# Feed-forward output of layer 0: where the seventh product's weights are added up, and where two bank copies and a table load stand

## The chip, the cores and the metric

The kernel runs on one core of one Trainium2 chip. The metric is the time of one execution on the device in microseconds; before the change the median of three runs is 1351.96 us (1351.9 to 1352.2). The profile is of one further execution, which took 1352.66 us; from its first to its last instruction (its span) it took 1350.7 us. Where a text says TensorE, VectorE, ScalarE, GpSimd and SyncE, the profile says PE (PEld for its weight loads), DVE, ACT, POOL and SP; a q behind the name is the engine's own instruction queue, which also issues transfers.

## The reference, cut to what matters

The program is a trunk of two layers for 256 latent tokens and 256 context tokens of width 1024. Each layer has a token mixer (an mLSTM in layer 0, latent attention in layer 1) and a gated feed-forward part; both are followed by a layer norm of the residual. The change is in the output product of the feed-forward part of layer 0 and at the norm behind it:

```python
def _conv_ffn(h, w_in, conv_w, conv_b, w_out):
    gate, up = jnp.split(h @ w_in, 2, axis=-1)
    return (jax.nn.silu(_dwconv(gate, conv_w, conv_b)) * up) @ w_out
...
f = _conv_ffn(_modulate(x, ml[3], ml[4]), ...)
x = _layer_norm(ALPHA * x + ml[5] * f, ln_g[i, 1], ln_b[i, 1])
```

w_out has 2816 rows and 1024 columns. The same is done for the context tokens, xc. All values are float32.

## The kernel before, in words

**Products in three passes.** A float32 operand is split into a high half, which ScalarE makes by a cast to fp32r, and a low half, which VectorE makes by subtracting the high half from the source. A product of two such operands is three matmuls: high by high, high by low, low by high (mm3, L420 to L427). In prod (L1655) the activations are the first operand, so the second matmul of each three (L426) is the first that needs the weights' low half.

**The weight stream.** Weights come in tiles of 128 rows by 1024 columns (512 KB). Class Stream goes through one fixed list of them (order, made by _plan). _load (L294) takes a raw buffer from a ring and issues the load on SyncE's queue; _split (L320) has ScalarE cast the tile into the high half (L342) and, through low (L362), VectorE subtract for the low half (L364), after which the raw buffer is given back and the next load is issued. use (L371) hands a tile to the products and first splits tiles ahead, as long as fewer than three (NB) of the w buffers are in use: the cast of a tile so waits until the tile three places ahead of it has been used up. From the first y tile on the ring has eleven raw buffers, from y22 on seven. SyncE works its queue in order; a load that waits for its buffer holds up all loads behind it.

**Seven products instead of eight.** The output product of layer 0 (w_fout0, L1629) is computed in blocks of 2 by 2: two blocks of weight rows in each pair, two halves of columns, two groups of 256 tokens, with seven block products and sums of operands on both sides. For each of six groups of rows (the last of half size, 512 columns) there are tiles yt2, y11, yt3, yt1, then in three more passes y21, y22 and yt4. The weights' sums are formed on the chip by _sum (L310): of the loaded tiles for yt3, yt1 and y11 VectorE makes T2 and the others in place (L316, L317, L318). T2 takes a raw buffer but no load. yt4 needs T4, the sum of T2 and B21 (the block that y21 also uses; ws holds it under yt4's number). So T2 is spilled: _split stores it into a tile of memory, t2d, by a transfer on ScalarE's queue (L344). When yt4's turn comes, _load reads t2d back on SyncE's queue (L302) and then adds B21 onto it by an accumulating transfer from GpSimd's queue (L303). The value projection of the mLSTM (w_v, tiles v...) does the same and keeps doing it.

**The activation side.** act_sums (L1607) is called for each of the eleven pairs of feed-forward rows, j = 0 to 10, while the input product (ffn_in, L1558) is still running. It forms sums, splits some of them, and stores the parts that are wanted later in a memory tile fd by two transfers on GpSimd's queue (L1618, L1624). In w_fout0 the step operand (L1638) brings them back: loads of 128 KB on ScalarE's queue (L1644, tile zr), and two steps later a cast on ScalarE (L1650) and a subtraction on VectorE (L1651, tile fz).

**The banks.** Four pairs of PSUM banks hold the running products: p6 (yt2), p1 (y11), p7 (yt3), p5 (yt1). When p1's six tiles are through, ScalarE copies its two banks into u1 (L1698); VectorE then adds p6 (L1705), adds the result to p7 (L1708) and so on (sums, L1703). p1 then takes y21, p5 takes y22, p7 takes yt4, each on top of what it holds. add (L1718) multiplies a finished bank by the gate, adds the residual z and takes statistics for the norm. z and the gate are loaded on GpSimd's queue (L1692, L1686). The norm of the context rows (z_norm, L1773) follows in the course of yt4: a square root on ScalarE (L1780), scaling on both engines (L1784, L1786), transposes on TensorE (L1271), then scale and shift and the split into hc (L1277, L1278, L1284, L1285), on which the first product of layer 1 (dkv, L1808) waits.

**What sets the order.** A planner takes the instructions as traced and gives each engine a fixed order: of the instructions that are ready by its own clock, the one traced first. Three helpers bind it. keep_in_program_order puts an instruction behind the last one traced so far on its engine. behind (L429) puts one behind named instructions of the same engine, in order only, without a wait for their end. st.behind lists instructions that the next splits must stand behind. Each transfer takes one of eight counters for those issued on SyncE's and ScalarE's queues, or one of eight for those on GpSimd's; an issue waits until the counter's last transfer has landed.

Of the kernel before, what the change touches and what calls it, by code (L numbers as in the profile page):

```python
# [10 lines left out]
AF = mybir.ActivationFunctionType  # L11
ALU = mybir.AluOpType
# [244 lines left out]
class Stream:  # L257
# [36 lines left out]
    def _load(self):  # L294
        k, j = self.k, self.nl
        key = self.order[j][0]
        n, cols = self.ids[key]
        j0, ring = self.ring(j)
        tag, bufs = ring[(j - j0) % len(ring)]
        t = k.pool.tile([128, CW], F32, tag=tag, name="raw", bufs=bufs)  # L300
        if key[0] in ("vt4", "yt4"):
            k.nc.sync.dma_start(t[:, :cols], k.t2d[key[0][0], key[1], key[2]][:, :cols])  # L302
            k.nc.gpsimd.dma_start(t[:, :cols], self.ws[n, :, :cols], accum_op=ALU.add)  # L303
        elif key[0] not in ("vt2", "yt2"):
            k.nc.sync.dma_start(t[:, :cols], self.ws[n, :, :cols])
        self.raw[j] = t
        self.tags[j] = tag
        self.nl += 1
# [11 lines left out]
    def _split(self):  # L320
        k, j = self.k, self.ns
        key, wide = self.order[j]
        cols = self.ids[key][1]
        while self.nl <= j:
            self._load()
        self.nsum = max(self.nsum, j)
        while self.nsum < min(j + SUMS, self.n):
            while self.nl <= self.nsum:
                self._load()
            self._sum(self.nsum)  # L330
            self.nsum += 1
        raw = self.raw[j]
        if wide:
            h, l = self.unit(), None
            if self.later is None:
                l = self.unit()
        else:
            w = k.pool.tile([128, 2, CW], F32R, tag="w", name="w", bufs=NB)
            h, l = w[:, 0], w[:, 1]
            self.live.append(j)  # L340
        src = raw[:, :cols]
        k.behind(k.nc.scalar.copy(h[:, :cols], src), self.behind)  # L342
        if key[0] in ("vt2", "yt2"):
            k.nc.scalar.dma_start(k.t2d[key[0][0], key[1], key[2]][:, :cols], src)  # L344
        self.hl[j] = [h, l]
        self.ns += 1
        if l is None:
            self.later.append((j, src, self.hl[j]))
        elif key[0] == "dkv" and key[2]:
            self.kept_low.append((j, src, h, l))  # L350
        else:
            self.low(j, src, h, l)
        while self._room():
            self._load()
# [39 lines left out]
class K:  # L394
# [1212 lines left out]
    def act_sums(self, j, x1, x2):  # L1607


        nc = self.nc  # L1610
        a, b = slice(0, 256), slice(256, 512)
        if j == 0:
            self.fa, self.fd = {}, []
        d = self.dr.tile([128, 768], F32, name="fd")
        t = self.s2("fs")
        nc.vector.tensor_sub(t[:, a], x1[:, b], x2[:, b])
        nc.vector.tensor_sub(t[:, b], t[:, a], x1[:, a])
        nc.gpsimd.dma_start(d[:, 0:512], x2)  # L1618
        nc.vector.tensor_sub(x1[:, b], x1[:, a], x1[:, b])
        u, v = self.u("fa"), self.u("fs")  # L1620
        self.split(u[:, 0], u[:, 1], x1)
        self.split(v[:, 0], v[:, 1], t)
        nc.vector.tensor_add(x1[:, a], x2[:, a], t[:, b])
        nc.gpsimd.dma_start(d[:, 512:768], x1[:, a])  # L1624
        self.fa["1", j], self.fa["S3", j] = u[:, :, a], u[:, :, b]
        self.fa["S1", j], self.fa["S2", j] = v[:, :, a], v[:, :, b]
        self.fd.append(d)

    def w_fout0(self, x1d, mid):  # L1629


        nc, st, A = self.nc, self.st, self.fa
        pin = self.tc.keep_in_program_order
        parts = [("2", i) for i in range(6)] + [("S4", i) for i in range(6)] + [("3", i) for i in range(6)]
        off = {"2": 0, "3": 256, "S4": 512}
        got = []

        def operand():  # L1638
            if parts:
                x, i = parts.pop(0)  # L1640
                r = self.s2("zr")
                js = [j for j in (2 * i, 2 * i + 1) if j < 11]
                for h, j in enumerate(js):
                    pin(nc.scalar.dma_start(r[:, h * 256:(h + 1) * 256], self.fd[j][:, off[x]:off[x] + 256]))  # L1644
                got.append((x, js, r))
            if len(got) > 2 or not parts and got:
                x, js, r = got.pop(0)
                n = 256 * len(js)
                u = self.u("fz")
                pin(nc.scalar.copy(u[:, 0, :n], r[:, :n]))  # L1650
                nc.vector.tensor_sub(u[:, 1, :n], r[:, :n], u[:, 0, :n])  # L1651
                for h, j in enumerate(js):
                    A[x, j] = u[:, :, h * 256:(h + 1) * 256]

        def prod(ps, x, w, i, bs=(0, 1), on=False):  # L1655
            for h in range(2 if i < 5 else 1):
                j = 2 * i + h
                a = A[x, j]
                for b in bs:
                    ts = slice(b * 128, (b + 1) * 128)  # L1660
                    cs = slice(h * 512, (h + 1) * 512)
                    self.mm3(ps[b], (a[:, 0, ts], a[:, 1, ts]), (w[0][:, cs], w[1][:, cs]), j == 0 and not on, j == 10, on)

        def pair():
            return [self.ps("y") for _ in range(2)]

        lo, hi = slice(0, 512), slice(512, 1024)
        p6, p1, p7, p5 = [pair() for _ in range(4)]
        n = 0
        u2 = []  # L1670
        for i in range(6):
            for name, ps, x in (("yt2", p6, "S2"), ("y11", p1, "1"), ("yt3", p7, "S3"), ("yt1", p5, "S1")):
                w = st.use((name, 0, i))
                prod(ps, x, w, i)
                for f in ("S2", "1", "S3", "S1"):
                    if f == x:
                        for j in (2 * i, 2 * i + 1):
                            A.pop((f, j), None)
                self.tick(1)
                if n >= 8:  # L1680
                    operand()
                if n == 14:
                    gate = []
                    for g in (1, 0):
                        t = self.uf("gate")
                        nc.gpsimd.dma_start(t, self.gd[0, 5][g:g + 1, :].to_broadcast([128, 1024]))  # L1686
                        gate.append(t)
                if n >= 16 and n % 2 == 0:
                    if n == 16:
                        z = []  # L1690
                    t = self.uf("z")
                    nc.gpsimd.dma_start(t, x1d[len(z)])  # L1692
                    z.append(t)
                n += 1
                if (name, i) == ("y11", 5):
                    for b in range(2):
                        u = self.s2("u1")
                        pin(nc.scalar.copy(u, p1[b]))  # L1698
                        u2.append(u)
        stats = [self.tiny(12, "st").rearrange("p (a b) -> p a b", b=6) for _ in range(4)]  # L1700
        vv = []

# [15 lines left out]
        def add(g, c, ps, bs=(0, 1)):  # L1718

            for b in bs:  # L1720
                t = self.s2("zp")
                zz = z[2 * g + b][:, c]
                nc.vector.tensor_tensor(t, ps[b], gate[g][:, c], op=ALU.mult)
                nc.vector.scalar_tensor_tensor(zz, zz, ALPHA, t, op0=ALU.mult, op1=ALU.add)
                nc.vector.bn_stats(stats[2 * g + b][:, c.start // 512], zz)
# [7 lines left out]
        for i in range(6):  # L1733
            w = st.use(("y21", 0, i))
            prod(p1, "2", w, i, on=True)
            self.tick(1)
            operand()
# [3 lines left out]
        for i in range(6):  # L1741
            w = st.use(("y22", 0, i))
            prod(p5, "S4", w, i, on=True)
            self.tick(1)
            operand()
        self.drain()
        add(0, hi, p5)
        self.bg = [mid(0, z[0:2], stats[0:2])]
# [514 lines left out]
```

## Time and profile before

| | us |
|---|---|
| median of three runs | 1351.96 |
| the profiled execution | 1352.66 |
| its span | 1350.7 |
| TensorE busy (matmuls) | 1338.8 |
| VectorE busy | 1058.7 |
| ScalarE busy | 711.3 |
| GpSimd busy | 124.7 |

In the profile a line of a group or of the timeline names the source line, the engine, the operation and what it writes and reads (out<-in), with sizes as partitions by elements. Timeline rows begin with the start and the duration in us, and end in brackets with the engine's idle time before the row and what ended it. Rows of waits give who waited for whom: us in total, times, longest. Rows of windows give a stretch, its length, and for each engine the busy time with the number of instructions in brackets, in the order PE, PEld, DVE, ACT, POOL; then the granted TensorE clock, the mean busy share of the sixteen DMA engines, and GB/s. Rows of the chain of waits give start, duration and what the end waited for. Rows of DMA issues give the number of transfers, the size of each, and the median time from issue to landing.

The input product of layer 0's feed-forward part runs up to 922 us, the products of w_fout0 from there to about 1038, interleaved at their end with the first products of layer 1.

### The profile page before, as it was taken

The page shows a single profiled execution, that of the slowest core. Times are in us where ns is not written, and L with a number is a line of the kernel's source. Part 1 is how long each engine was busy: PE and PEld are TensorE (multiplying, and loading weights), DVE is VectorE, ACT ScalarE, POOL GpSimd, SP SyncE. Part 2 cuts the span into 40 slices and gives each one's busy share as a digit, 9 for nine tenths or more (in the row PEclk, how much of TensorE's full clock was granted, in tenths as well). Part 3 has the DMA queues.
Part 4 walks back from the last instruction along what each step waited for, and adds up shares of the span by engine and source line. Part 5 has one row for each costly group of instructions (what it writes and reads, how often), then busy time and mean ns, then how long its engine had stood idle before and what let it go on. Part 6 is the DMA issues. An engine that isn't in the chain of part 4 may idle for free.

```text
span 1350.7 us, 18775 instructions
## 1 busy us (share of the span) xinstructions
PE 1338.8 (99%) x6662; PEld 1120.2 (83%) x6662; DVE 1058.7 (78%) x1748; ACT 711.3 (53%) x1251; POOL 124.7 (9%) x218
## 2 busy tenths in 40 slices
PE   9999999999999999999999999999999999999997
PEld 6777888888888888888898888888878998988886
DVE  4798656677688697897979878767899788898873
ACT  4765544445734545464643433334557767676660
POOL 0222000011101011030002000000001002000100
PEclk9999999999999999999999999999999999999999
DMA  9888848789676374785627876645987437366750
GB/s 362 323 278 283 281 162 257 229 280 311 217 251 195 95 248 137 239 300 198 232 84 245 296 244 229 221 142 206 310 255 243 157 102 211 134 210 190 257 193 32
DMA packets 92637, 298.26 MB, mean 221 GB/s; under 512 B 12120, under 2 KB 16472, under 8 KB 92544
## 3 DMA queue, kind: packets, MB, share of 16 engines
q1 hardware_dynamic: 62992, 218.65, 48.5%
q0 software_dynamic: 17888, 58.09, 13.8%
q10 hardware_dynamic: 11664, 20.32, 4.2%
q8 instruction: 52, 0.85, 0.3%
q14 instruction: 41, 0.34, 0.1%
HBM read 263.56 MB, written 33.46 MB: 220 GB/s over the span
## 4 chain that ended last, share of the span: by engine, by line
PE 93%; DMA 3%; DVE 1%; ACT 1%; issue 1%; ACTq 0%; DVEq 0%; POOL 0%; POOLq 0%; SPq 0%
PE fin L1472 8%; PE tok L423 6%; PE fin L423 6%; PE fin L426 6%; PE fin L427 6%; PE tok L426 6%; PE tok L427 6%; PE y L426 5%; PE y L427 5%; PE y L423 5%; PE qk L423 4%; PE qk L427 4%; PE qk L426 4%; PE up L709 2%; DMA raw<-in_ws 2%; PE up L423 1%
## 5 line engine op out<-in xcount | busy, mean ns | idle before, releaser
L342 ACT CAST w<-raw 128x1024 fp32r<-128x1024 f32 (+2 forms) x286 | 296.2, 1037 | 289.7 <-PE fin L427 78.9
L364 DVE TENSOR_TENSOR w<-raw,w 128x1024 fp32r<-128x1024 f32 (+2 forms) x286 | 343.2, 1203 | 133.4 <-ACT w L342 127.8
L537 DVE SCALAR_TENSOR_TENSOR junk<-ar,bc 128x1024 f32<-128x1024 f32 x128 | 155.9, 1218 | 5.0 <-ACT bc L579 3.0
L426 PE MATMUL fin<-h,w 128*128 128x512 f32 (+1 forms) x376 | 141.2, 376 | 0.0
L427 PE MATMUL fin<-h,w 128*128 128x512 f32 (+1 forms) x376 | 140.9, 375 | 0.0
L423 PE MATMUL fin<-h,w 128*128 128x512 f32 (+1 forms) x376 | 140.8, 376 | 0.1
L1472 PE MATMUL fin<-h,w 128*128 128x512 f32 (+1 forms) x636 | 111.1, 337 | 0.0
L1472 PEld LDWEIGHTS fin<-h,w 128*128 128x128 f32 x636 | 97.6, 190 | 13.2
L423 PE MATMUL qk<-xc,w 128*128 128x512 f32 x256 | 100.6, 393 | 0.0
L427 PE MATMUL qk<-xc,w 128*128 128x512 f32 x256 | 99.9, 390 | 0.0
L426 PE MATMUL qk<-xc,w 128*128 128x512 f32 x256 | 99.8, 390 | 0.0
L426 PEld LDWEIGHTS fin<-h,w 128*128 128x128 f32 x376 | 70.8, 188 | 13.1 <-DVE h L1304 0.2
L427 PEld LDWEIGHTS fin<-h,w 128*128 128x128 f32 x376 | 70.8, 188 | 12.8
L423 PEld LDWEIGHTS fin<-h,w 128*128 128x128 f32 x376 | 70.5, 188 | 13.0 <-ACT h L1303 0.3
L427 PEld LDWEIGHTS qk<-xc,w 128*128 128x128 f32 x256 | 48.1, 188 | 9.9
L426 PEld LDWEIGHTS qk<-xc,w 128*128 128x128 f32 x256 | 48.1, 188 | 9.7
L423 PEld LDWEIGHTS qk<-xc,w 128*128 128x128 f32 x256 | 48.1, 188 | 9.7
L423 PE MATMUL tok<-w,hT 128*128 128x512 f32 x128 | 49.9, 390 | 0.0
L426 PE MATMUL tok<-w,hT 128*128 128x512 f32 x128 | 49.8, 389 | 0.0
L427 PE MATMUL tok<-w,hT 128*128 128x512 f32 x128 | 49.8, 389 | 0.0
L726 ACT ACTIVATE fg<-fg 128x512 f32<-128x512 f32 (+1 forms) x44 | 23.1, 525 | 45.5 <-DVE fg L724 39.4
L364 DVE TENSOR_TENSOR wu<-raw,wu 128x1024 fp32r<-128x1024 f32 (+1 forms) x37 | 43.7, 1201 | 3.6 <-ACT wu L342 3.2
(481 smaller groups left out, 3109.2 us busy)
## 6 DMA issues: line engine op xcount, KB each, us to landing
raw<-in_ws SPq DMA_DIRECT2D x282, 512.0 KB, 4.4
ar<-in_adaT SPq DMA_DIRECT2D x80, 512.0 KB, 4.7
adaw<-in_ada SPq DMA_DIRECT2D x16, 512.0 KB, 8.0
t2d<-raw ACTq DMA_DIRECT2D x13, 512.0 KB, 6.0
raw<-t2d SPq DMA_DIRECT2D x13, 512.0 KB, 6.4
raw<-in_ws POOLq DMA_DIRECT2D x13, 512.0 KB, 8.3
zr<-fd ACTq DMA_DIRECT2D x33, 128.0 KB, 4.4
xmd<-xr POOLq DMA_DIRECT2D x16, 256.0 KB, 4.9
```

Of the source, the lines that this page charges most:

```text
L342: k.behind(k.nc.scalar.copy(h[:, :cols], src), self.behind)
L364: i = self.k.nc.vector.tensor_sub(l[:, :n], src, h[:, :n])
L423: q = mm(out, w[0], x[0], start=start, stop=False, skip_group_check=on)
L426: mm(out, w[0], x[1], start=False, stop=False, skip_group_check=on)
L427: mm(out, w[1], x[0], start=False, stop=stop, skip_group_check=on)
L537: nc.vector.scalar_tensor_tensor(o, w, 1.0, self.bc[j], op0=ALU.mult, op1=ALU.mult, accum_out=col[:, k, j:j + 1])
L709: nc.tensor.matmul(ps[m], wk[i][:, c], hT[k][:, j], start=made[m] == 0, stop=made[m] == 23)
L726: nc.scalar.activation(tmp[:, :n], tmp[:, :n], AF.Silu)
L1472: self.nc.tensor.matmul(ps[:, 0:256] if x else ps, w[x][:, k * 128:(k + 1) * 128], h[:, 0:256] if x else h, start=i == 0 and not k0, stop= ...
```

## The change

In _load a yt4 tile is read by one plain load of its t2d tile. In _split the spill of a yt2 tile becomes an accumulating transfer from GpSimd's queue onto t2d. So that there is something to add to, act_sums copies B21, memory to memory, from ws to t2d on GpSimd's queue, in its calls j = 5 to 10 (for yt4's tiles 0 to 5), each pinned behind what GpSimd's queue has so far. The v tiles keep the old way.

The two copies of p1's banks are traced after st.use of tile yt3 5, whose splits hold the cast of y21's tile 0, and no longer ahead of it. And a square root of a constant into an unused tile is put on ScalarE behind the last cast of operand; the table for square roots is loaded with it.

```diff
         t = k.pool.tile([128, CW], F32, tag=tag, name="raw", bufs=bufs)
-        if key[0] in ("vt4", "yt4"):
+        if key[0] == "yt4":
+            k.nc.sync.dma_start(t[:, :cols], k.t2d["y", key[1], key[2]][:, :cols])
+        elif key[0] == "vt4":
             k.nc.sync.dma_start(t[:, :cols], k.t2d[key[0][0], key[1], key[2]][:, :cols])
             k.nc.gpsimd.dma_start(t[:, :cols], self.ws[n, :, :cols], accum_op=ALU.add)
...
         k.behind(k.nc.scalar.copy(h[:, :cols], src), self.behind)
-        if key[0] in ("vt2", "yt2"):
+        if key[0] == "yt2":
+            k.nc.gpsimd.dma_start(k.t2d["y", key[1], key[2]][:, :cols], src, accum_op=ALU.add)
+        elif key[0] == "vt2":
             k.nc.scalar.dma_start(k.t2d[key[0][0], key[1], key[2]][:, :cols], src)
...
         nc.gpsimd.dma_start(d[:, 512:768], x1[:, a])
+        if j > 4:
+            n, cols = self.st.ids["yt4", 0, j - 5]
+            self.tc.keep_in_program_order(
+                nc.gpsimd.dma_start(self.t2d["y", 0, j - 5][:, :cols], self.st.ws[n, :, :cols]))
...
-        got = []
+        got, cut = [], []
...
                 u = self.u("fz")
-                pin(nc.scalar.copy(u[:, 0, :n], r[:, :n]))
+                cut[:] = [nc.scalar.copy(u[:, 0, :n], r[:, :n])]
+                pin(cut[0])
...
                 w = st.use((name, 0, i))
+                if (name, i) == ("yt3", 5):
+                    for b in range(2):
+                        u = self.s2("u1")
+                        pin(nc.scalar.copy(u, p1[b]))
+                        u2.append(u)
                 prod(ps, x, w, i)
...
                 n += 1
-                if (name, i) == ("y11", 5):
-                    for b in range(2):
-                        u = self.s2("u1")
-                        pin(nc.scalar.copy(u, p1[b]))
-                        u2.append(u)
...
             operand()
+        self.behind(nc.scalar.activation(self.tiny(1, "pre"), self.keps, AF.Sqrt), cut)
         self.drain()
         add(0, hi, p5)
```

## The prediction, made before the result was known

> **What bounds the kernel now.** I read the page's busy shares first, then TensorE's own waits, then windows around them, and last the rows of each engine there.
>
> ```profile
> span 1350.7 us, 18775 instructions
> PE 1338.8 (99%) x6662; PEld 1120.2 (83%) x6662; DVE 1058.7 (78%) x1748; ACT 711.3 (53%) x1251; POOL 124.7 (9%) x218
> PE idle L646 <- DVE adav L490: 1.5, 1, 1.5
> PE y L426 <- DVE w L364: 1.0, 1, 1.0
> PE dkv L423 <- ACT hc L1284: 0.8, 1, 0.8
> 940.00:980.00 40.00, 40.00 (x178) 33.14 (x177) 32.70 (x37) 20.81 (x28) 1.62 (x3) 1.00 0.88 305
> 980.00:985.00 5.00, 3.99 (x18) 2.98 (x17) 5.00 (x9) 4.83 (x8) 0.00 (x0) 1.00 0.98 334
> 985.00:1020.00 35.00, 35.00 (x156) 28.93 (x155) 31.48 (x43) 17.37 (x22) 3.89 (x5) 1.00 0.86 249
> 1023.00:1025.00 2.00, 1.20 (x10) 0.96 (x9) 0.93 (x3) 1.97 (x5) 0.00 (x0) 1.00 1.00 244
> 1340.00:1350.70 10.70, 2.75 (x23) 2.54 (x22) 6.75 (x15) 0.44 (x2) 2.85 (x2) 0.83 0.26 98
> ```
>
> TensorE is busy 1338.8 of 1350.7 us. Of the 11.9 us left, 8.0 lie in the tail after 1340 and most of the rest at the start. The change works between about 820 and 1030, where only two waits of TensorE exist: **1.01 us** at 983 (5.00 less 3.99), for the low half of a weight tile, and **0.80 us** at 1024 (2.00 less 1.20), for a high half of the context activations. A change that adds no matmul and removes none can gain these 1.81 us at most, 0.13% of the time. What a measurement of this kernel can tell from no change is about 0.2%, 2.7 us. So a gain that counts isn't there to be had; the open questions are how much of 1.81 comes, and whether something new is late. The profiled execution took 1352.66 us for a span of 1350.7, 0.70 over the median of 1351.96; I take differences from its rows and put them on the median.
>
> **The first wait: the bank copies.** ScalarE and VectorE around it, then TensorE:
>
> ```profile
> 980.07 0.58 ACT L1698 COPY u<-y 128x512 f32<-128x512 f32 x1
> 980.54 0.58 ACT L1698 COPY u<-y 128x512 f32<-128x512 f32 x1
> 981.02 1.06 ACT L342 CAST w<-raw 128x1024 fp32r<-128x1024 f32 x1
> 982.49 1.05 ACT L342 CAST w<-raw 128x1024 fp32r<-128x1024 f32 x1
> 980.91 1.28 DVE L1705 TENSOR_TENSOR u<-y,u 128x512 f32<-128x512 f32 x2
> 982.11 0.69 DVE L1708 TENSOR_TENSOR y<-y,u 128x512 f32<-128x512 f32 x1
> 982.71 1.22 DVE L364 TENSOR_TENSOR w<-raw,w 128x1024 fp32r<-128x1024 f32 x1
> 983.84 0.68 DVE L1651 TENSOR_TENSOR fz<-zr,fz 128x512 fp32r<-128x512 f32 x1
> 983.98 0.50 PE L426 MATMUL y<-w,fz 128*128 128x512 f32 x1 [1.01 <-DVE w L364]
> ```
>
> The cast at 981.02 is y21's tile 0; two copies of p1 stand ahead of it. Moved ahead of them it starts at 980.07 and ends at 981.13, and its subtraction (1.22) can end at 982.35, before TensorE asks for it at 982.97 (983.98 less 1.01). The copies then end at about 982.1, where the cast's end was, so the next cast stays at 982.49. But VectorE has no idle time here (5.00 of 5.00), and the same work must still be done before tile 1's subtraction: L1705 twice, two L1708, one L1651. In the present order that next subtraction comes last and ends at 986.3 (983.84 and two pieces of 0.6 and 1.22 behind it). TensorE asks for it one tile after 982.97 or a little sooner: twelve matmuls at 40.00 us by 178, so 2.7, at about 985.3 to 985.7. So the wait can come back one tile later, up to 1.0 us, if the planner leaves that subtraction last; each 0.6 us piece that falls behind it takes 0.6 off. Bounds of the gain: 0 and 1.01. I take half, **-0.5**, since the subtraction is traced ahead of those pieces but its cast ends only at 983.54.
>
> **The second wait: table, and the two-step loads of T4.** The chain of waits, ScalarE, GpSimd and the page's DMA list:
>
> ```profile
> 1006.02 10.29 DMA raw<-in_ws
> 1016.41 1.95 ACT L342 CAST w<-raw 128x1024 fp32r<-128x1024 f32 x2 [2.24 <-DMA raw<-in_ws]
> 1018.38 1.28 ACT L1780 ACT_TABLE_LOAD   x1
> 1024.02 0.71 ACT L1284 CAST hc<-zm 128x256 fp32r<-128x256 f32 x2
> t2d<-raw ACTq DMA_DIRECT2D x13, 512.0 KB, 6.0
> raw<-t2d SPq DMA_DIRECT2D x13, 512.0 KB, 6.4
> raw<-in_ws POOLq DMA_DIRECT2D x13, 512.0 KB, 8.3
> 1006.02 0.87 POOL L303 DMA_DIRECT2D raw<-in_ws  x1 [0.41 <-DVE w L364]
> 1019.62 2.01 POOL L303 DMA_DIRECT2D raw<-in_ws  x2 [0.39 <-issue]
> ```
>
> A T4 tile now needs a load of T2 (6.4) and, behind it, an accumulating load of B21 (8.3); the third lands at 1016.3 and holds ScalarE's cast for 2.24. Then a table load of 1.28 us stands ahead of the square root, and everything up to the cast of hc at 1024.02 follows in line. After: six accumulating loads leave, and one load of 6.4 us from SP's same six places brings T4 ten microseconds sooner; the cast is then limited by its weight buffer, from about 1013. The table load, with a dummy square root of 0.3, moves behind the last L1650 cast, into the stretch where ScalarE idles (17.37 busy of 35.00 between 985 and 1020). If that cover were gone it would cost 1.6 us of ScalarE there, inside the lead of a cast worked out below. So hc comes at least 1.28 earlier by the table alone, more than the 0.80 that TensorE waits; next late would be TensorE's own transposes, which is no wait. Bounds 0 (if the cast or dkv's casts take the freed place) and 0.80; I take **-0.8**, since two independent removals each exceed it or come near it.
>
> [...]
>
> **The spill: ScalarE's store becomes GpSimd's accumulation.** Rows:
>
> ```profile
> SPq L305 <- DMA t2d<-raw: 34.1, 5, 9.2
> ACT fz L1650 <- DMA raw<-in_ws: 3.5, 2, 2.5
> 961.89 6.15 DMA t2d<-raw
> 968.10 4.40 DMA raw<-in_ws
> 972.52 0.33 ACTq L1644
> 978.89 11.20 SPq L305 DMA_DIRECT2D raw<-in_ws  x6
> 994.74 1.05 ACT L342 CAST w<-raw 128x1024 fp32r<-128x1024 f32 x1 [1.31 <-PE y L427]
> ```
>
> Removed: six issues of 0.33 on ScalarE's queue. Added: six of about 0.87 on GpSimd. No row shows an accumulation into memory; the nearest, into the chip, takes 8.3 against the store's 6.0. I bound it by 6.0 and by 10.3, the slowest row above, and take 8.3, so +2.3 each. Behind it waits SP, in order, since the raw buffer comes free only then: 34.1 us in five waits now, some 46 then. Behind SP's waiting load stand the other loads. They have room: the load issued at 978.89 is y22's first, its cast is at 994.74, and its landing takes about 5, leaving ten. The weak place is the other one: at 972.52 an issue of zr on ScalarE's queue waited until a load of SP had landed that itself had waited for the spill, and the L1650 cast behind it lost 2.5 us. What is +2.3 for the spill can so be +2.3 for ScalarE. Its lead: with three weight buffers a cast starts two tiles (5.4 us) before use and needs 1.06 and 1.22 with the subtraction, which leaves 3; in the last row of half tiles the same gives 1.4; I take 2. Against that, six 6 us transfers leave the queues that zr shares. I count 0 and keep 0 to +2.3 per spill for the rivals. DMA share in that stretch is 0.88 already, so the added traffic pushes it towards 1.
>
> [...]
>
> **The copies of B21.** Six issues on GpSimd, each behind the second store of its L1607 call:
>
> ```profile
> 793.22 0.54 POOL L1618 DMA_DIRECT2D fd<-fg  x1 [16.27 <-DVE fg L1594]
> 929.84 0.54 POOL L1624 DMA_DIRECT2D fd<-fg  x1 [5.54 <-DVE fg L1623]
> 944.96 0.54 POOL L1692 DMA_DIRECT2D z<-x1d  x1 [10.04 <-PE y L427]
> 700.00:900.00 200.00, 200.00 (x884) 165.61 (x883) 162.11 (x257) 77.38 (x133) 15.13 (x28) 1.00 0.71 232
> 973.34 0.33 ACTq L344 DMA_DIRECT2D t2d<-raw  x1
> ```
>
> GpSimd idles 16 us between calls and DMA has 0.29 free. Memory to memory isn't shown; between the 6.4 of a plain load and 10.3 it lands long before its spill: the last is issued after 929.84 for a spill at 973.34. Queued behind the last copy are the gate and z loads, which are used only after the y21 loop, near 998. Cost 0. The spills now stand in the same queue as the z loads, which wait for buffers, 10.04 us in the row above; a spill behind such a load would be late by as much, and SP with it. The planner takes the one that is ready first, so I count 0 for it, and put it with the slower rival.
>
> **Sum.** -0.5 - 0.8 = -1.3: 1351.96 - 1.3 = **1350.7 us** (on the profiled execution, 1351.4).
>
> **Rivals.**
> 1. *VectorE takes the first gain back and more*, or zr lands up to 1 us later: first wait 1 to 2 us, second gone. 1351.96 + 0 to 1.0 - 0.8 = 1351.2 to 1352.2. For it: VectorE 5.00 of 5.00. Against: zr loses the stores ahead of it.
> 2. *Slower: the accumulating spill holds ScalarE.* The last three spills each delay, through SP's load, a zr issue by 2.3 to 4.3 us; once the lead of 2 is gone TensorE pays: 3 x 2.3 - 2 = 4.9, less 0.8 = +4.1, 1356.1; at 4.3 each 10.9 - 0.8, 1362. It decides from a spill landing of 8 us or more if the same zr follows. For it: the rows at 961.89 to 972.52, and DMA at 0.88. Against: the planner spreads loads and zr anew, and between spills ScalarE idles half the time.
> 3. *It doesn't do what it says*: a copy, cast or table load is placed so that both waits stay, 1352.0.
> 4. *More than the waits comes*: nothing in the rows gives over 1.8; some reordering near 1130 or in the tail would have to, 1349.
>
> **Chances.** Forecast (1350.0 to 1351.2) 0.50; rival 1 0.20; rival 2 0.20; rival 3 0.08; more than 2.7 us faster 0.02. Faster by over 0.2% 0.02, within 0.78, slower 0.20. The range runs from all of 1.81 gained less the 0.2 by which single runs differ, 1349.9, up into the lower part of rival 2, where only some of the spills get through, 1355.0; what it leaves out is the rest of rival 2 and rival 4.
>
> **What would show it.** Right: no wait for L1284 near 1023, ACT_TABLE_LOAD before 1000, T4's casts waiting for TensorE instead of DMA, the first wait under 0.6 or moved one tile on. Wrong: TensorE waiting for L364 or L1651 between 945 and 985, ScalarE's waits for raw<-in_ws above 3.5, SP's waits for the spill far above 46, landings of the spill above 10.

## The result, and the profile after

| | before | after |
|---|---|---|
| median, us | 1352.08 (6 runs, 1351.9 to 1353.17) | 1359.84 (6 runs, 1358.97 to 1360.81) |
| the profiled execution, us | 1352.66 | 1358.97 |
| its span, us | 1350.7 | 1356.6 |

The changed kernel is slower: ratio **1.0053**, 95% interval 1.0042 to 1.0063, or 7.8 us between the medians. The prediction was 1350.7 us.

Windows of the changed kernel, with the same columns and mostly the same bounds as those shown of before:

```profile
940.00:980.00 40.00, 38.98 (x173) 31.97 (x171) 29.84 (x33) 18.05 (x23) 5.82 (x9) 1.00 0.98 292
970.00:980.00 10.00, 8.98 (x40) 7.12 (x39) 5.64 (x9) 3.69 (x6) 2.48 (x4) 1.00 1.06 375
980.00:985.00 5.00, 3.67 (x12) 1.92 (x12) 1.88 (x3) 1.14 (x2) 0.00 (x0) 1.00 1.03 401
985.00:990.00 5.00, 2.86 (x7) 2.06 (x8) 3.02 (x5) 3.83 (x7) 0.00 (x0) 0.74 0.91 279
987.00:991.00 4.00, 3.70 (x9) 2.70 (x10) 3.32 (x5) 3.69 (x7) 0.00 (x0) 0.57 0.88 262
990.00:1020.00 30.00, 30.00 (x131) 24.45 (x130) 28.06 (x38) 17.28 (x23) 0.00 (x0) 0.99 0.72 223
1023.00:1025.00 2.00, 2.00 (x10) 1.65 (x9) 2.00 (x5) 1.27 (x2) 0.00 (x0) 1.00 0.37 124
```

And two of the kernel before, for 970 to 980 and 987 to 991:

```profile
987.00:991.00 4.00, 4.00 (x19) 3.30 (x19) 3.95 (x5) 3.05 (x5) 0.00 (x0) 1.00 0.89 295
970.00:980.00 10.00, 10.00 (x46) 8.29 (x45) 7.63 (x13) 5.11 (x10) 0.00 (x0) 1.00 0.86 305
```

Nearly the whole loss lies between 978 and 991. From 940 to 1020 the kernel before ran 178 + 18 + 156 = 352 matmuls, the changed one 173 + 12 + 7 + 131 = 323. The 29 that are missing are 6.5 us at 40.00 us by 178. The second wait (1023 to 1025, now 2.00 of 2.00 busy) gives 0.8 back, which leaves 5.7; the spans differ by 5.9. VectorE and ScalarE, full before at 980 to 985 (5.00 and 4.83), are busy 1.88 and 1.14 of 5.00 there: they wait too. Only the DMA engines are fuller: 1.06 and 1.03 against 0.86 and 0.98 (the profile's mean share can pass 1).

TensorE's rows after its waits, changed kernel; in the brackets the idle time and what ended it:

```profile
979.83 0.50 PE L427 MATMUL y<-w,fa 128*128 128x512 f32 x1 [1.02 <-ACT w L344]
...
986.84 0.51 PE L427 MATMUL y<-w,fs 128*128 128x512 f32 x1 [2.21 <-ACT w L344]
987.65 0.79 PE L430 MATMUL y<-w,fs 128*128 128x512 f32 x1 [0.30 <-DVE w L368]
```

With three more of 0.31 to 0.33 these are 4.5 us of waiting, for ScalarE's casts and behind them VectorE's subtractions. After the wait of 2.21 the granted clock is 0.5 for 3.4 us (0.57 in the row for 987 to 991, 9 matmuls in place of 19), worth some 1.7 us. Less the 1.0 us that the kernel before waited there, waits and half clock make 5.2 of the 6.5 us; the rest is not told apart, but the first matmul behind each wait is listed with 0.50 us or so, against 0.22 for a usual one. ScalarE in turn:

```profile
969.83 0.62 ACT L1658 CAST fz<-zr 128x512 fp32r<-128x512 f32 x1 [2.11 <-DMA zr<-fd]
...
973.68 0.62 ACT L1658 CAST fz<-zr 128x512 fp32r<-128x512 f32 x1 [2.27 <-DMA zr<-fd]
...
978.64 0.62 ACT L1658 CAST fz<-zr 128x512 fp32r<-128x512 f32 x1 [3.81 <-DMA raw<-in_ws]
...
985.65 0.62 ACT L1658 CAST fz<-zr 128x512 fp32r<-128x512 f32 x1 [3.33 <-DMA zr<-fd]
```

All four are casts of zr (L1650 before). The wait of 3.81 ended with a weight load because the zr issue ahead of the cast stood until that load had landed: in the trace both use the same one of the eight counters. The chain of waits names the links:

```profile
962.35 7.71 DMA t2d<-raw
970.11 0.33 SPq L307
970.53 7.61 DMA raw<-in_ws
978.22 7.35 DMA zr<-fd
985.65 0.63 ACT fz L1658
...
987.65 0.79 PE y L430
```

The fifth of the six spills lands, SyncE's waiting load goes, the zr issue waits until that load has landed, and zr takes 7.35 us. That is the chain of rival 2, but the last two transfers are slow too. What crowds them stands on GpSimd's queue. Before:

```profile
930.54 1.09 POOL L1686 DMA_DIRECT2D gate<-gd  x2 [0.16 <-issue]
...
955.84 0.54 POOL L1692 DMA_DIRECT2D z<-x1d  x1 [3.54 <-ACT fz L1650]
```

After:

```profile
962.35 0.85 POOL L346 DMA_DIRECT2D t2d<-raw  x1 [11.63 <-DVE raw L319]
963.07 1.24 POOL L1700 DMA_DIRECT2D gate<-gd  x2
964.18 0.65 POOL L1706 DMA_DIRECT2D z<-x1d  x1
973.82 0.89 POOL L346 DMA_DIRECT2D t2d<-raw  x1 [8.99 <-DMA zr<-fd]
974.38 1.92 POOL L1706 DMA_DIRECT2D z<-x1d  x3
```

The gate and z loads, six of 512 KB, were spread over 930 to 956. Now GpSimd's fixed order has five of the six spills ahead of the first of them (the fifth is the row at 962.35), and they leave in a bunch at 963 to 976. The list of DMA issues between 925 and 990 of the changed kernel (number, size, median us to landing):

```profile
t2d<-raw POOLq DMA_DIRECT2D x4, 512.0 KB, 7.0
z<-x1d POOLq DMA_DIRECT2D x4, 512.0 KB, 10.9
gate<-gd POOLq DMA_DIRECT2D x2, 512.0 KB, 9.1
```

A z load takes 10.9 us, against 5.2 in the same list of before. So there are two suspects: the **bunch**, by which gate and z loads at 963 to 976 are meant, and the **accumulating spill** that holds up SyncE. In the experiments the first theory says that the bunch is the cause, the second that the spill's longer stay is.

### The profile page after: what moved, and what is told of

The parts are those of the page before. It is cut to its first block, busy times and chain, and to the rows that moved or that the text cites. A ratio compares the mean times of both kernels' runs of the same rounds, so it can differ in the third digit from the quotient of the medians.

```text
span 1356.6 us, 18767 instructions
## 1 busy us (share of the span) xinstructions
PE 1341.2 (99%) x6662; PEld 1120.8 (83%) x6662; DVE 1058.2 (78%) x1748; ACT 712.0 (52%) x1252; POOL 127.6 (9%) x224
## 4 chain that ended last, share of the span: by engine, by line
PE 93%; issue 2%; DMA 2%; DVE 1%; ACT 1%; POOL 0%; SPq 0%; DVEq 0%; ACTq 0%; POOLq 0%
PE fin L1476 8%; PE tok L427 6%; PE fin L427 6%; PE fin L430 6%; PE fin L431 6%; PE tok L431 6%; PE tok L430 6%; PE y L430 5%; PE y L427 5%; PE y L431 5%; PE qk L427 4%; PE qk L431 4%; PE qk L430 4%; PE up L713 2%; PE up L427 1%
```

## The experiments

Each ratio is against runs of the kernel before on the same chip (medians there 1352.2 to 1352.8 us).

| run | what it is | us | ratio, 95% interval |
|---|---|---|---|
| e3 | spill part of the change alone | 1359.58 | 1.0054 [1.0039, 1.0069] |
| e4 | bank copies and table alone | 1352.80 | 1.0002 [0.9993, 1.0012] |
| e2 | before, plain spill on GpSimd's queue | 1360.15 | 1.0055 [1.0040, 1.0070] |
| e5 | e2, gate and z early | 1352.38 | 0.9995 [0.9985, 1.0004] |
| e1 | changed kernel, gate and z early | 1356.33 | 1.0028 [1.0016, 1.0039] |
| e10 | e3, gate and z early | 1355.72 | 1.0020 [1.0009, 1.0031] |
| e9 | e1, spill overwrites | 1351.67 | 0.9991 [0.9981, 1.0000] |
| e7 | changed kernel, zr a step earlier | 1358.93 | 1.0043 [1.0029, 1.0057] |
| e6 | e1, zr a step earlier | 1352.04 | 0.9994 [0.9985, 1.0003] |
| e11 | bank copies alone | 1353.68 | 1.0006 [0.9996, 1.0015] |
| e12 | table alone | 1352.46 | 1.0000 [0.9990, 1.0009] |
| e8 | e4, zr a step earlier | 1352.01 | 0.9996 [0.9987, 1.0005] |
| e13 | e5, bank copies and table | 1353.09 | 1.0003 [0.9994, 1.0011] |
| e14 | e6, bank copies at their old place | 1354.58 | 1.0014 [1.0005, 1.0023] |

### Which part: e3 and e4

e3 has the first three hunks of the diff (load, spill, copies of B21), e4 the others (bank copies, table).

```diff
-        if key[0] in ("vt2", "yt2"):
+        if key[0] == "yt2":
+            k.nc.gpsimd.dma_start(k.t2d["y", key[1], key[2]][:, :cols], src, accum_op=ALU.add)
+        elif key[0] == "vt2":
...
```

> The kernel before with the T2 and T4 part of the change alone; bank copies and table load stay where they were. Both theories: as slow as the changed kernel or slower, 1359 to 1361. If the moved copies or the table load do the harm, 1350 to 1353.

> The kernel before with the moved bank copies and the early table load alone. Both theories: 1350.4 to 1351.5, the second wait of TensorE gone (-0.8), the first halved (-0.5) if the loads of T4 don't hold it back. If these two parts do the harm: 1356 or more.

e3 loses 7.2 us, nearly all of it. e4 missed the 1350.4 to 1351.5 that was expected by both theories: its interval holds no change and reaches down to a gain of 0.9 us, short of the 1.3 of the sum.

### The bunch: e2, e5 and e1

e2 is the kernel before with nothing but the queue of T2's plain store changed: no accumulation, no copy of B21, T4 in two steps.

```diff
-        if key[0] in ("vt2", "yt2"):
+        if key[0] == "yt2":
+            k.nc.gpsimd.dma_start(k.t2d["y", key[1], key[2]][:, :cols], src)
+        elif key[0] == "vt2":
             k.nc.scalar.dma_start(k.t2d[key[0][0], key[1], key[2]][:, :cols], src)
```

> The kernel before, with T2's plain store moved from ScalarE's to GpSimd's queue and nothing else: no accumulation into memory, no copies, T4 still added up on the way back. GpSimd's queue then has gate and z where the changed kernel has them. Bunching theory: slower by 4 to 8 us, 1356 to 1360. Spill theory: a store of the same bytes and about the same 6 us, so 1351.5 to 1353.

It loses 7.8 us. Its spills land in 2.9 to 5.8 us, sooner than the 6.0 of before, and its gate and z loads stand behind the fifth spill as in the changed kernel. So the change of queue alone is enough for the whole loss. e5 (on e2) and e1 (on the changed kernel) trace the gate loads and the z loads earlier, so that they stand ahead of most spills:

```diff
-                if n == 14:
+                if n == 1:
...
-                if n >= 16 and n % 2 == 0:
-                    if n == 16:
+                if n in (4, 6, 8, 10):
+                    if n == 4:
```

> The kernel before, with T2's plain store on GpSimd's queue (no accumulation, no copy of B21) and the gate and z loads traced early, as in e1. If what e1 still loses (about 4 us) is the accumulation's longer landing, this run has none of it: 1352 to 1353. If it is the spill's place on GpSimd's queue, whatever the transfer is, this run loses the same as e1: 1355.5 to 1357.5. If the loads taken early were not the cause in e1 at all, it loses what e2 lost: 1359 to 1360.5.

> The changed kernel, with the two gate loads and the four z loads traced 12 or 13 tiles sooner, so that GpSimd's queue has them ahead of the third T2 spill (the last z ahead of the fourth) instead of behind the fourth and fifth. Bunching theory (gate and z, 3 MB, go out at 963 to 987 with the zr loads, zr lands late, ScalarE is late): back to 1350 to 1352, TensorE idle for L344 gone. Spill theory (the accumulating spill itself holds SyncE's loads and so ScalarE): stays at 1357 or more, since all six spills are unchanged.

e5 loses nothing. Windows of e2, then of e5:

```profile
970.00:980.00 10.00, 9.50 (x42) 7.32 (x41) 5.12 (x8) 2.48 (x5) 2.15 (x4) 1.00 1.05 403
```

```profile
970.00:980.00 10.00, 10.00 (x46) 8.26 (x44) 6.64 (x10) 4.68 (x9) 0.55 (x1) 1.00 0.87 300
```

Between e2 and e5 only the place of six loads in the traced order differs, and it is worth 1.0055 against 0.9995: **the place of the gate and z loads is shown as a cause**. It is the place, not that they leave close together: in e5 five of the six leave between 925 and 933, closer than in the changed kernel, and TensorE doesn't wait there. e1 gets back only half of its loss, as neither theory had it (1356.33, expected 1350 to 1352 or 1357 and more). Its gate and z loads leave at 925 to 934 and 950, yet TensorE has one wait of 2.09 us at 983, and the chain of waits of e1 has the links of the changed kernel with shorter loads:

```profile
964.63 7.55 DMA t2d<-raw
972.24 0.33 SPq L307
972.66 5.03 DMA raw<-in_ws
977.76 6.03 DMA zr<-fd
983.87 0.63 ACT fz L1658
```

### The accumulation: e9 and e10

e9 is e1 with the one operand taken away that makes the spill add. T4 is then T2 without B21; all transfers stay.

```diff
-            k.nc.gpsimd.dma_start(k.t2d["y", key[1], key[2]][:, :cols], src, accum_op=ALU.add)
+            k.nc.gpsimd.dma_start(k.t2d["y", key[1], key[2]][:, :cols], src)
```

> e1 with one thing changed: the spill from GpSimd's queue overwrites t2d with T2 in place of adding to it. It so leaves out B21 in T4, and its copies of B21 are made for nothing. If the accumulation's longer stay is what e1 still loses, nothing is left of it: 1351.5 to 1353, spills landing about 1 us sooner and no half clock near 987. If it is the copies of B21, T4's one load on SyncE's queue or the later bank copies, 1355.5 to 1357.

> The change's spill part alone (copies of B21, accumulating spill, one plain load of T4) with the gate and z loads traced early; bank copies and table as before. If the accumulating spill by itself costs the rest of e1: 1355.5 to 1357, a ScalarE wait of over 3 us for zr and a TensorE wait of about 2 us near 984. If the later bank copies or the table load have a part in it: 1352 to 1354.

e10 is e3 with e1's edit. It loses 2.9 us, so the bank copies and the table aren't needed for the rest of the loss. e9 loses nothing: with six transfers that overwrite in place of adding, e1's 1.0028 becomes 0.9991, some 5 us. The list of DMA issues between 925 and 990, first of e1, then of e9:

```profile
t2d<-raw POOLq DMA_DIRECT2D x4, 512.0 KB, 7.2
```

```profile
t2d<-raw POOLq DMA_DIRECT2D x4, 512.0 KB, 4.8
```

SyncE's waits for the spill between 925 and 1035, e1 and then e9 (total, times, longest):

```profile
SPq L307 <- DMA t2d<-raw: 27.9, 4, 8.6
```

```profile
SPq L307 <- DMA t2d<-raw: 18.1, 4, 7.0
```

An accumulating spill lands 2.4 us later than an overwriting one from the same queue, and SyncE's four waits are 2.4 us longer on average. It also fills the DMA engines longer: between 925 and 990 the transfers of GpSimd's queue took 36.1% of the sixteen engines' time in e1 and 28.4% in e9, for the same 6.16 MB. Which of the two makes zr late, the wait or the fuller engines, these runs don't separate. So **each of the two causes is enough alone** (e2: the loads' late place without accumulation, 7.8 us; e1 and e10: accumulation without it, 4.0 and 2.9), and together they cost no more than the first.

### The last link: e7 and e6

Both issue each zr load one operand step earlier, which is one weight tile or 2.7 us (the first zr load leaves at 942.2 in e7 and at 944.9 in the changed kernel) and not the 5 us that the expectations give; e7 is the changed kernel with this edit, e6 is e1 with it.

```diff
-            if len(got) > 2 or not parts and got:
+            if len(got) > 3 or not parts and got:
...
-                if n >= 8:
+                if n >= 7:
```

> The changed kernel with only the zr loads one operand step earlier; the gate and z loads stay bunched behind the spills. If the bunched loads act through zr alone, most of the 7.5 us goes: 1352 to 1355. If they act through the weight loads as well, 1356 to 1358. If zr is no link, 1359 to 1360.5.

> The changed kernel with the gate and z loads traced early and each zr load issued one operand step earlier (about 5 us). If ScalarE's late casts of zr are the last link of all that is lost, the rest of e1 goes: 1351 to 1353, and no half clock near 987. If another wait carries the rest (the weight loads of SyncE, VectorE's subtractions), it stays at 1355.5 to 1357.

In e6 the rest of the loss is gone though the spills still accumulate and land no sooner (median 8.2 us, 7.2 in e1): late zr loads are the link through which they harm. In e7 little comes back, against my first guess: 6.1 us are still lost. Its chain of waits:

```profile
962.27 8.04 DMA t2d<-raw
970.36 6.35 DMA raw<-in_ws
976.78 9.37 DMA rope<-in_rope
986.16 0.33 ACTq L1652
```

With the bunch on the way other loads land late as well, here a rope load of 9.37 us, and the next zr issue on ScalarE's queue stands until 986.16 for it. Here asking earlier doesn't help, since the issue itself is held.

### The two waits that were to go: e11, e12, e8, e13 and e14

e11 moves the bank copies only, e12 loads the table early only; the edits are the last hunks of the change's diff.

> The kernel before with only the two bank copies traced behind y21 tile 0's cast. By the prediction's first term the wait of 1.01 us at 983 shrinks or moves one tile on, by 0.5 in all: 1351.8. By rival 1 VectorE, full there, gives it all back as one or more waits between 981 and 988: 1352.2 to 1353. The second wait (0.80 at 1024) stays by both.

> The kernel before with only the square-root table loaded early. By the prediction's second term the wait of 0.80 us at 1024 goes and the first wait (1.01) stays: 1351.5. If the two-step loads of T4 alone hold the second wait, 0.5 to 0.8 of it stays: 1352.3.

TensorE's waits between 925 and 1035, e11, then e12, then e4:

```profile
PE dkv L423 <- ACT hc L1284: 0.9, 1, 0.9
PE y L426 <- DVE w L364: 0.2, 1, 0.2
```

```profile
PE y L426 <- DVE w L364: 0.6, 1, 0.6
```

```profile
PE y L426 <- DVE w L364: 0.5, 1, 0.5
```

The table load alone takes the second wait away. The copies alone shrink the first to 0.2, but it is 0.6 without moving them (e12) and 0.5 with both (e4): it moves by some tenths whatever is changed nearby. e11's median is above both expectations and e12's near the second, but both intervals hold no change: the times can't tell these apart.

e8 is e4 with e6's edit for zr. e13 is e5 with bank copies and table. e14 is e6 with the copies put back:

```diff
-                if (name, i) == ("yt3", 5):
+                if (name, i) == ("y11", 5):
                     for b in range(2):
...
```

> The kernel before with the two parts of the change that cost nothing (bank copies later, square-root table early) and the zr loads one operand step earlier. If zr stands behind the small waits of e4 between 980 and 988, they go with it: 1350.3 to 1351.5. If those waits are VectorE's own work, it is as e4: 1352 to 1353. The earlier zr loads may cost a wait elsewhere: above 1353.

> e5 (plain store on GpSimd's queue, T4 in two steps, gate and z loads early) with the later bank copies and the early table load. It differs from e9 only in how T4 is read back and in the copies of B21, and it computes the reference. If the accumulation into memory was the whole rest of e1, it is as e9: 1351.3 to 1352.3, ratio 0.999 to 1.0. If e9 gained from T4's one load, it stays at e5's 1352.4 or over.

> e6 (the changed kernel, gate and z loads early, zr one step earlier) with the bank copies at their old place. In e6 TensorE waits 0.6 us for the moved copies at 983 and 0.5 for a low half at 987. If the copies' new place is worth something, this run has the old wait of 1.0 us or more for the low half near 983 and is as e6 or slower: 1352.0 to 1353. If the new place only trades one wait for others, it is the same within 0.5 us: 1351.5 to 1352.5.

e8 and e13 are as the kernel before. e13 is 0.8 us over what was expected if it were as e9, and lies where it was expected if e9 gained from T4's one load. Its runs spread from 1351.27 to 1354.25, its profiled one (span 1349.9) has one wait of 0.4, and what the longer runs wait for isn't shown. So whether T4's one load is worth the 1.4 us between e13 and e9 stays open, since the two intervals overlap. e14 missed too: it is 2.5 us over e6 (1.0014 against 0.9994). With accumulating spills the old place of the copies does cost: 0.8 us more of waiting (1.9 against 1.1 in e6) and a half clock worth 1.7. TensorE's waits in e14:

```profile
PE y L427 <- ACT w L344: 1.0, 1, 1.0
PE y L430 <- DVE w L368: 0.9, 1, 0.9
```

Those two, at 983 and 985, are followed by 3.4 us of half clock. No version that computes the reference was measurably faster than the kernel before; e6, the changed kernel with both cures, equals it.

## Why the prediction was wrong

**What bounds the kernel** held: at most 1.8 us could be gained, and no version's median was more than 1.1 us under the kernel before.

**The second wait, -0.8:** the mechanism was right. The wait is gone in the changed kernel, in e4 and in e12. In the changed kernel's ScalarE rows the table load stands at 1000.98, behind the last cast of zr as I wanted it (my sign was before 1000, but the kernel is late by then), and T4's casts wait for TensorE. That the 0.8 us comes off the time is not shown: e12, where only this was changed, measures 1.0000, with an interval of 0.9990 to 1.0009 that would allow it.

**The first wait, -0.5:** mis-sized at best. In e4 0.5 of it is left at 987, one to two tiles later, which is the half that I took; but e12 leaves 0.6 without the move, so little of it is the copies' doing there. e14 shows a worth of the move that I had not counted: 2.5 us, 1.7 of them half clock, where ScalarE is late.

**The copies of B21, 0:** the copies themselves cost nothing that e9 shows, since it makes them all for no use and isn't slower than before. The step that failed is the sentence behind it: "Queued behind the last copy are the gate and z loads, which are used only after the y21 loop, near 998. Cost 0." I asked when these loads are used, and not when they would be on the way. They did come in time for their users. But they came behind five spills, into a stretch where the DMA share was 0.86 before and rose to 1.06, and slowed zr. I had looked at the other order (a spill behind a z load) and counted 0 because "the planner takes the one that is ready first". The gate loads left at 930.54 before, and behind the spill of 962 after; the profile doesn't show why the planner ordered them so. This is the 7.8 us of e2.

**The spill, counted 0, rival 2 at a chance of 0.20:** the mechanism of rival 2 was there as written (spill, SyncE's load, zr issue, cast, TensorE) and its price came out near: +4.1 forecast, 4.0 measured in e1 and 2.9 in e10. That agreement is in part luck. The forecast was waiting alone; e1 has 3.1 us of it between 925 and 1035, and a half clock worth 1.7 us for which I had no term. The longer stay was mis-sized too: I added 2.3 us per spill to the old store and so expected SyncE to wait 46 us for spills instead of 34.1. The changed kernel's row for 900 to 1040:

```profile
SPq L307 <- DMA t2d<-raw: 40.0, 5, 12.3
```

That is 1.2 us for each of five waits. The 2.4 us between e9 and e1 are measured against another thing, an overwriting store on GpSimd's queue, which lands sooner (4.8) than the old one on ScalarE's (6.0). Also off is the point from which it decides. I asked for landings of 8 us; in e1 the median was 7.2, and in the changed kernel 7.0. TensorE's waits of the changed kernel begin at the half tiles, for which I had worked out a lead of 1.4 us before taking 2 for all. And the 0 was a choice between 0 and +2.3 per spill that no row of before supported; e1 and e10 show 4.0 and 2.9 us in its place.

**The copies' landing** added nothing, as forecast: the spills waited for VectorE's sum (11.63 us in the row at 962.35) and once for a load of zr (8.99 in the row at 973.82), never for a copy.

## What to carry to other kernels

A transfer that is moved to another queue must be costed with everything that will stand behind it there: ask when those transfers will then be on the way and what else the DMA engines carry at that time, not only whether they arrive in time for their users. A transfer that holds a buffer for which an in-order load queue waits counts with its full stay (7.71 us at 962.35 in the changed kernel), and the first to be late may be a small load on a third queue that shares a counter with a load of that queue (there zr, 128 KB, issued only at 978.22). To tell such causes apart, undo each alone in the changed kernel: here either one was enough for a loss, so that removing one showed half of it and removing the last link in the wrong version showed little.

## What the runs showed of the hardware

**An accumulating transfer into memory.** 512 KB from the chip onto memory landed in 7.2 us (median, e1), an overwriting one from the same queue in 4.8 (e9); its issue took GpSimd 0.85 to 0.90 us (e1) against 0.53 to 0.54 (e2). A copy of B21 from memory to memory took 3.7 us for 256 KB at 931 in the changed kernel.

**Half clock after a short stall.** After waits of 2.21 us (changed kernel), 2.09 (e1) and 2.41 (e2) the granted clock was 0.5 for 3.4 us; after 2.45 (e7) for 6.8; after 1.1 (e5) and after 1.92 (e10) not at all. In e14 two waits of 1.00 and 0.89 were enough. So the length of one wait doesn't decide. What does is seen in the trace's records of the clock: it is first granted in full at 4.37 us in the changed kernel, 5.61 in the kernel before and 6.38 in e14, and each later change of the first two, as well as the fall in e14, lies a whole multiple of 3.413 us, the length of the changed kernel's record at half clock, behind that moment (changed kernel: 987.41, which is 288 times 3.4133; before: 1347.05, 393 times; e14: 986.00, 287 times). Windows of e14, e7 and e10 that begin and end at such multiples:

```profile
982.59:986.00 3.41, 1.52 (x6) 0.71 (x5) 3.41 (x5) 3.41 (x6) 0.00 (x0) 1.00 0.90 325
986.00:989.41 3.41, 3.41 (x10) 2.63 (x9) 3.41 (x5) 1.31 (x2) 0.00 (x0) 0.50 0.87 242
```

```profile
984.11:987.53 3.42, 1.56 (x6) 0.86 (x5) 0.83 (x2) 1.00 (x2) 0.00 (x0) 1.00 1.06 387
```

```profile
980.59:984.00 3.41, 2.52 (x11) 1.73 (x10) 0.89 (x2) 0.15 (x1) 0.00 (x0) 1.00 0.99 306
984.00:987.41 3.41, 2.07 (x7) 1.20 (x8) 2.91 (x6) 3.41 (x7) 0.00 (x0) 1.00 0.86 241
```

e14 and e7 have 1.89 and 1.86 us of idle time inside one such window, and the clock falls at its end. In e10 the wait of 1.92 is cut by a boundary at 984.00, which leaves 0.89 and 1.34, and it doesn't fall. In the traces of before and of the changed kernel, cut at such multiples, tails included, no window at full clock with at most 1.27 us of idle time (977.17 to 980.59, changed kernel) was followed by a fall, and those with 2.27 (984.00 to 987.41, changed kernel) and 3.41 (one in each tail) were. In e7 the window behind the fall was idle for another 0.89 us, and the half clock stayed for a second window. So 1.86 us of idle time in a window of 3.41 were enough in these runs, and 1.34 were not. The prediction had no term for the half clock, and its 1.7 us are more than either wait that the change was to remove.
